# Positions on chip ordered by residue modulo 16, token order restored at the write of the mixed values; the far blocks of pattern 16 transposed in place by VectorE

## The chip, the cores and the metric

One Trainium2 chip, one of its cores. The metric is the device time of one execution in microseconds. TensorE (PE) multiplies; its weight loads are listed apart as PEld. VectorE is DVE, ScalarE is ACT, GpSimd is POOL; all DMAs are issued from SyncE's queue (SP).

## What is computed

One decoder layer on 2048 positions of width 1024, in float32. After a norm, one projection gives q, k, v and a gate for 12 heads of width 64, and four parts for a short convolution:

```python
h = rmsnorm(x, norm_pre_g)
z = einsum('bsd,de->bse', h, w_in)
q, k = rope(q, pos), rope(k, pos)
for window, dilation in ((128, 1), (512, 4), (2048, 16)):
    # regrouped by residue mod dilation: query i sees keys i-128 .. i of its own residue
    o_i, lse_i = dilated_window_attn(q, k, v, window, dilation)
mix_w = softmax(stack(lses), axis=0)
attn_out = sum(mix_w * outs) * silu(g_attn)
conv_out = c_b * causal_depthwise_conv(c_c * c_h, conv_w) * silu(g_conv)
y = concat([attn_out, conv_out]) @ w_out
x = x + rmsnorm(y, norm_post_g)
```

So a query at token t sees three sets of keys: all of the last 129 tokens (pattern 1), every fourth of the last 513 (pattern 4), and every sixteenth of all earlier ones (pattern 16).

## The kernel before, in words

**Tiling.** The 2048 positions are four blocks b of 512 (`NB`, `C`). The columns of the projection are eight groups of 512: groups 0 and 7 are the convolution, groups 1 to 6 are one pair of heads each. One unit n is one group on one block, so there are 32 units, group by group and b from 0 to 3 within each. After them an output projection runs in eight steps with seven products each (L1008 to L1010). Each float32 product is three matmuls of float32r parts, high by high, high by low and low by high; a "part" is made by an ACT copy and a DVE subtraction.

**Positions.** Inside a block the 512 positions stand by residue modulo 4: place = 128 r + i for token 4 i + r (`order`, L52). For pattern 4, residue r is then a contiguous run of 128 places. Pattern 16 lives inside the same score blocks: of the keys of residue r, those with (q - k) % 4 == 0 belong to pattern 16 too (`four`, L60). Patterns 4 and 16 are computed together as kind 4; pattern 1 is kind 1.

**One attention unit** (`attn_unit`, L533). k and q are scaled out of PSUM (L547), their halves are swapped by four small DMAs (L550), and they are rotated by DVE and POOL (L562, L566). k goes to the long-lived tiles `KK` in two parts (L572, L573), q to `Q` (L577, L578); POOL writes a copy `Q1` of q in token order for kind 1 (L582). v is transposed on PE (L594), kept by residue as `V2` and, through two DMAs by way of DRAM (L607, L610), by token as `V1`. `score4` (L623) multiplies `Q` of residue r by all keys of that residue so far, 128 (b + 1) columns; `score1` (L648) multiplies 128 queries of `Q1` by 256 keys that it reads in pieces out of `KK` (L658). DVE adds the mask and takes the row minimum in one pass (L638, L666), ACT does the exponential (L642, L670).

Then `probs` (L677) takes probabilities in groups of up to four 128 x 128 blocks: four PE transposes into PSUM (L684), an ACT copy (L689) and a DVE subtraction (L690) into the tile `pt`, and PE multiplies by v (L703). `gather` (L712) brings the products out of PSUM (L721 to L723). The row minima and sums of kind 1 go through DRAM to the other order (L758, L760); small DVE steps (L769 to L785) make the weights, which go through DRAM to all partitions (L788, L791). DVE weighs both kinds (L807, L808), POOL adds them and multiplies by the gate (L809, L810), and a DMA writes the result to `mix_d` (L811), from where the output projection loads it.

Kind 4 has 4 (b + 1) blocks per head, 40 over the four b; of them 4 (b - 1) for b > 1 lie at least two blocks back. In these far blocks (c < b - 1) every key within pattern 4's window is too old, and only pattern 16 is left: a probability is not zero only where (q - k) % 4 == 0.

**Order.** Nothing is ordered by hand. Every step is given to `Plan` with an engine, an assumed duration, a priority, and what it reads and writes; `Plan.schedule` runs through assumed time and gives each engine the first step that is ready and finds its buffer, and `emit` writes the instructions in that order. A changed step can so move any other. Steps marked `port` are planned so that none of them on DVE stands beside one on POOL. Buffers are rings: `z` (3 PSUM banks, projection), `st` (5 PSUM banks, everything else of attention), `pt` (3), `uu` (4), `u` (1), `xt` (9) and others.

Of the kernel before, what the change touches and what calls it, by code (L numbers as in the profile page):

```python
# [40 lines left out]
def _constants():  # L42
# [18 lines left out]
    tok = (np.arange(128) % 32) * 4 + np.arange(128) // 32  # L61
# [221 lines left out]
def dvet(n):  # L283
    return n / 960.0 + 0.067
# [11 lines left out]
def hybrid_layer(ctx: ExitStack, tc: tile.TileContext, x, w_in, w_out, conv_w, g_pre, g_post,  # L296
# [19 lines left out]
    cst = cp.tile([128, 7 * 128], F32, name="cst")  # L316
    ident, mask1, mask4 = cst[:, 0:128], cst[:, 128:384], cst[:, 384:896]
# [6 lines left out]
    e_d = [dram.tile([4, 32, 4, 4], F32, name=f"ed{i}") for i in range(2)]  # L324
    a_d = [dram.tile([32, 4, 128], F32, name=f"ad{i}") for i in range(2)]
# [24 lines left out]
    KK = [ap_.tile([128, 4, NB * 128], F32R, name=f"kk{i}") for i in range(2)]  # L350
# [65 lines left out]
    def x_chunk(b):  # L416
# [19 lines left out]
        for kt in range(KT):  # L436
# [56 lines left out]
    U, T_last = {}, None  # L493

    def conv_unit(n, i, b, zs):
# [16 lines left out]
        add("DVE", 0.25, pe, lambda: vec.tensor_copy(u.ap[:, 0:2, 1:], u.ap[:, 4:6, 0:127]), r=[(u, 1)], w=[(u, 2)])  # L512
# [12 lines left out]
        add("DVE", dvet(C) + 0.07, pr, lambda: vec.scalar_tensor_tensor(g.ap, y.ap, 0.5, g.ap, op0=ALU.mult, op1=ALU.mult),  # L525
            r=[y], w=[g], port=True)
# [6 lines left out]
    def attn_unit(n, p, b, zs):  # L533
# [89 lines left out]
        def score4(r0):  # L623
# [24 lines left out]
        def score1(g0):  # L648
# [28 lines left out]
        def probs(h, kind, blk, O):  # L677
            ps, pt = Tok(st_r), Tok(pt_r)
            m = len(blk)
            pp = P[h, kind]  # L680

            def tr():
                for i, (a, c) in enumerate(blk):
                    nc.tensor.transpose(ps.ap[:, i * 128:(i + 1) * 128], pp.ap[:, a, c * 128:(c + 1) * 128], ident)  # L684
            add("PE", 0.111 * m, pr, tr, r=[(pp, a) for a in sorted({a for a, _ in blk})] + ["cst"], w=[ps, (pt, "hold")])

            def p4():
                return ps.ap[:, :m * 128].rearrange("p (i c) -> p i c", c=128)
            add("ACT", actt(m * 128, True), pr + URG, lambda: act.copy(pt.ap[:, :m, 0, :], p4()), r=[ps], w=[(pt, 0)])  # L689
            add("DVE", dvet(m * 128), pr + URG, lambda: vec.tensor_tensor(  # L690
                pt.ap[:, :m, 1, :], p4(), f(pt.ap[:, :m, 0, :]), op=ALU.subtract), r=[ps, (pt, 0)], w=[(pt, 1)])

            def pv(part):
                for i, (a, c) in part:
                    dst = O[a // 2].ap.rearrange("p (l q) -> p l q", l=2)[:, :, (a % 2) * 128:(a % 2 + 1) * 128]
# [9 lines left out]
            for half in range(2):  # L705
                part = [(i, ac) for i, ac in enumerate(blk) if ac[0] // 2 == half]
# [408 lines left out]
```

## Time and profile before

| | us |
|---|---|
| median of 3 runs | 1218.31 |
| the runs | 1217.93, 1218.31, 1219.98 |
| the profiled execution | 1222.89 |
| its span, first to last instruction | 1220.8 |

The profile is of one execution, and its span is 2.1 us shorter than that execution's device time. Terms of a sum come from the span; a change of the span is then taken off the median of the runs. Matmuls are pipelined, so their listed durations overlap: a stream of them is read by the distance from start to start.

### The profile page before, as it was taken

How to read it: one execution, taken by the hardware profiler on the slowest of the kernel's cores; microseconds unless marked ns; L12 is line 12 of the kernel's file. 1: busy time of each engine (PE TensorE's matmuls, PEld its weight loads, DVE VectorE, ACT ScalarE, POOL GpSimd, SP SyncE). 2: the span in 40 equal slices, each digit the busy share in tenths (PEclk: the TensorE clock that was granted, in tenths of full speed). 3: DMA queues.
4: the chain of work that ended last, by engine and by line, in shares of the span. 5: the costliest groups of instructions: out<-in, count | busy, mean ns of one | idle time of the engine just before them, and what ended most of it. 6: DMA issues, size and time to landing. Idle time of an engine off the chain costs nothing.

```text
span 1220.8 us, 20955 instructions
## 1 busy us (share of the span) xinstructions
PE 1201.8 (98%) x6856; PEld 993.4 (81%) x6856; DVE 916.0 (75%) x2287; ACT 717.9 (59%) x1874; POOL 260.1 (21%) x212
## 2 busy tenths in 40 slices
PE   8999999999999999999999999999999999999997
PEld 6888888888878888788887888788888888777886
DVE  5556477877777787787788867787877759988876
ACT  6533447767557676576667676486676553454443
POOL 0011123322322232222332223222323113000000
PEclk9999999999999999999999999999999999999999
DMA  9989777766777657766877748767678779555452
GB/s 342 343 317 338 269 232 236 234 205 200 240 252 245 205 182 261 240 184 209 260 223 254 243 119 269 232 234 248 199 233 280 213 229 302 174 163 175 136 181 86
DMA packets 155884, 280.39 MB, mean 230 GB/s; under 512 B 31872, under 2 KB 90368, under 8 KB 155776
## 3 DMA queue, kind: packets, MB, share of 16 engines
q1 hardware_dynamic: 155776, 279.06, 69.6%
q8 instruction: 54, 0.88, 0.3%
q14 instruction: 54, 0.44, 0.1%
HBM read 215.36 MB, written 51.05 MB: 218 GB/s over the span
## 4 chain that ended last, share of the span: by engine, by line
PE 84%; DVE 8%; DMA 3%; ACT 2%; issue 1%; SPq 1%; DVEq 0%; ACTq 0%
PE z L848 16%; PE z L850 16%; PE z L849 16%; PE st L703 8%; PE st L684 7%; PE st L631 4%; PE st L659 3%; PE st L1010 2%; PE st L1008 2%; PE st L1009 2%; DMA rp<-rp 1%; PE z L1008 1%; PE z L1010 1%; PE z L1009 1%; ACT p L642 1%
## 5 line engine op out<-in xcount | busy, mean ns | idle before, releaser
L848 PE MATMUL z<-xt,w 128*128 128x512 f32 x960 | 397.1, 414 | 0.0
L850 PE MATMUL z<-xt,w 128*128 128x512 f32 x960 | 377.7, 393 | 0.0
L849 PE MATMUL z<-xt,w 128*128 128x512 f32 x960 | 376.4, 392 | 0.0
L850 PEld LDWEIGHTS z<-xt,w 128*128 128x128 f32 x960 | 180.5, 188 | 40.3
L848 PEld LDWEIGHTS z<-xt,w 128*128 128x128 f32 x960 | 181.2, 189 | 32.7 <-issue 3.4
L849 PEld LDWEIGHTS z<-xt,w 128*128 128x128 f32 x960 | 181.5, 189 | 25.8
L690 DVE TENSOR_TENSOR pt<-st,pt 128x512 fp32r<-128x512 f32 x216 | 142.3, 679 | 48.1 <-ACT pt L689 46.2
L642 ACT ACTIVATE p<-p,sm 128x128 f32<-128x128 f32 (+3 forms) x192 | 105.9, 555 | 73.2 <-DVE sm L638 72.9
L689 ACT CAST pt<-st 128x512 fp32r<-128x512 f32 x216 | 120.0, 579 | 36.0 <-PE st L684 34.1
L703 PEld LDWEIGHTS st<-pt,v 128*128 128x128 f32 x852 | 121.5, 190 | 18.2 <-DVE pt L690 4.9
L703 PE MATMUL st<-pt,v 128*128 128x256 f32 x852 | 133.1, 287 | 2.0 <-DVE pt L690 1.9
L684 PE MATMUL st<-cst,p 128*128 128x128 f32 x852 | 123.1, 275 | 2.4 <-DVE sm L638 1.0
L723 DVE TENSOR_TENSOR uu<-st,uu 64x256 f32<-64x256 f32 x192 | 80.0, 421 | 57.1 <-ACT uu L722 53.5
L684 PEld LDWEIGHTS st<-cst,p 128*128 128x128 f32 x852 | 100.6, 141 | 22.8 <-issue 3.2
L752 POOL TENSOR_TENSOR uu<-uu 128x512 f32<-128x512 f32 x48 | 72.4, 1509 | 209.1 <-DVE uu L723 207.4
L638 DVE CUSTOM_DVE_ANT_0 p<-st,cst 128x128 f32<-128x128 f32 (+3 forms) x192 | 81.8, 487 | 46.7 <-PE st L631 46.4
L721 ACT COPY uu<-st 64x256 f32<-64x256 f32 x192 | 70.2, 368 | 58.7 <-PE st L703 52.3
L670 ACT ACTIVATE p<-p,e 128x256 f32<-128x256 f32 (+1 forms) x192 | 94.9, 499 | 12.4 <-DVE e L666 12.3
L562 POOL TENSOR_TENSOR rp<-rp,cs 128x512 f32<-128x512 f32 x24 | 35.3, 1472 | 225.7 <-DMA rp<-rp 145.4
L666 DVE CUSTOM_DVE_ANT_0 p<-st,cst 128x256 f32<-128x256 f32 (+1 forms) x192 | 66.8, 411 | 20.5 <-PE st L659 20.4
L562 DVE TENSOR_TENSOR rp<-rp,cs 128x512 f32<-128x512 f32 x72 | 55.9, 791 | 23.4 <-DMA rp<-rp 23.0
L722 ACT COPY uu<-st 64x256 f32<-64x256 f32 x192 | 69.6, 367 | 3.2 <-DVE uu L723 0.4
(320 smaller groups left out, 1842.7 us busy)
## 6 DMA issues: line engine op xcount, KB each, us to landing
xt<-xt SPq DMA_DIRECT2D x256, 512.0 KB
cs<-t SPq DMA_DIRECT2D x28, 768.0 KB
raw<-in_w_in SPq DMA_DIRECT2D x59, 256.0 KB
rp<-rp SPq DMA_DIRECT2D x192, 64.0 KB
vd<-v SPq DMA_DIRECT2D x96, 128.0 KB
v<-vd SPq DMA_DIRECT2D x24, 512.0 KB
ab<-ad SPq DMA_DIRECT2D x48, 256.0 KB
mix<-g SPq DMA_DIRECT2D x32, 256.0 KB
```

The lines of the kernel that those rows point to most:

```text
L562: add(e, dur, pr, lambda o=o, a=a, i=i, eng=eng: eng.tensor_tensor(o.ap, a.ap, cs.ap[:, i], op=ALU.mult), r=[cs], w=[o], port=True)
L638: add("DVE", dvet(w) + 0.01, pr + URG, lambda h=h, r=r, P4=P4: vec.tensor_tensor_reduce(P4.ap[:, r, 0:w], ps[h].ap[:, (r - r0) * w:(r - r0 ...
L642: add("ACT", actt(w) + 0.19, pr, lambda h=h, r=r, P4=P4: act.activation(P4.ap[:, r, 0:w], P4.ap[:, r, 0:w], AF.Exp, bias=s4(0, h)[:, r:r + ...
L670: add("ACT", actt(256 - lo[g]) + 0.19, pr, lambda h=h, g=g, P1=P1: act.activation(P1.ap[:, g, lo[g]:], P1.ap[:, g, lo[g]:], AF.Exp, bias=E ...
L684: nc.tensor.transpose(ps.ap[:, i * 128:(i + 1) * 128], pp.ap[:, a, c * 128:(c + 1) * 128], ident)
L689: add("ACT", actt(m * 128, True), pr + URG, lambda: act.copy(pt.ap[:, :m, 0, :], p4()), r=[ps], w=[(pt, 0)])
L690: add("DVE", dvet(m * 128), pr + URG, lambda: vec.tensor_tensor(pt.ap[:, :m, 1, :], p4(), f(pt.ap[:, :m, 0, :]), op=ALU.subtract), r=[ps, ...
L703: mm(dst, v, pt.ap[:, i], start=s, stop=e)
L723: add("DVE", dvet(256), pr + URG, lambda: vec.tensor_tensor(cols(a, lo), o()[lo:lo + 64, 0], cols(a, lo), op=ALU.add), r=[O], w=[(a, (h, h ...
L848: mm(z.ap, w.ap[:, 0, js], xt.ap[:, 0], start=kt == 0, stop=False)
L849: mm(z.ap, w.ap[:, 0, js], xt.ap[:, 1], start=False, stop=False)
L850: mm(z.ap, w.ap[:, 1, js], xt.ap[:, 0], start=False, stop=kt == KT - 1)
```

## The change

The 512 places of a block now stand by residue modulo 16 inside residue modulo 4: token 16 a + 4 s + r stands at place 128 r + 32 s + a (a from 0 to 31). The order comes in with the PE transposes of x, whose identity operand becomes the permutation `perm`. The constants grow by these 128 columns, and the first load of them brings 256 columns where it brought 128.

In a far block, query and key of one residue modulo 16 now lie in one 32 x 32 square on the block's diagonal, and all else is zero. `probs` is split into `parts` and `times`. For far blocks `parts` has DVE transpose the 32 x 32 squares in place in SBUF, which transposes the whole block; the ACT copy and the DVE subtraction then read SBUF instead of PSUM, and no PSUM bank is taken. Near blocks keep the PE transposes. For b > 1, `times` multiplies all blocks of one half of O at once.

```diff
-    order = np.arange(C).reshape(128, 4).T.reshape(-1)
+    order = np.arange(C).reshape(32, 4, 4).transpose(2, 1, 0).reshape(-1)
...
-    KK = [ap_.tile([128, 4, NB * 128], F32R, name=f"kk{i}") for i in range(2)]
+    KK = [ap_.tile([128, 16, NB * 32], F32R, name=f"kk{i}") for i in range(2)]
...
-                nc.tensor.transpose(ps.ap[:, i * 128:(i + 1) * 128], xn[i].ap[:, kt * 128:(kt + 1) * 128], ident)
+                nc.tensor.transpose(ps.ap[:, i * 128:(i + 1) * 128], xn[i].ap[:, kt * 128:(kt + 1) * 128], perm)
...
+    def placed(t):
+        return t.rearrange("p (r s a) -> p r s a", r=4, s=4)
+    def natural(t):
+        return t.rearrange("p (r a s) -> p r s a", r=4, s=4)
...
-        g = silu2(zs[3], t, pe)
+        g = silu2(zs[3], t, pe, natural, placed)
...
-        add("POOL", poolt(C), pr, lambda: pool.tensor_tensor(y.ap, y.ap, bb.ap, op=ALU.mult), r=[bb], w=[y], port=True)
+        add("POOL", poolt(C) + 0.2, pr, lambda: pool.tensor_tensor(natural(yn()), placed(y.ap), placed(bb.ap), op=ALU.mult), r=[y, bb], w=[u], port=True)
...
+        def rows(t):
+            return t.rearrange("p (x g a) -> p g x a", x=16, g=4)
+        def tokens(t):
+            return t.rearrange("p (g x a) -> p g x a", g=4, x=16)
...
+        add("DMA", dmat(512), pr, lambda: nc.sync.dma_start(
+            d.rearrange("r p c -> p r c"), f(v2.ap).rearrange("p r k d -> p r (k d)")), r=[v2], w=[dk], land=3.8)
         for g in range(4):
             add("DMA", 0.5, pr, lambda g=g: nc.sync.dma_start(
-                d[g].rearrange("(r j) c -> j r c", r=4), f(v2.ap[32 * g:32 * g + 32]).rearrange("j r k d -> j r (k d)")),
-                r=[v2], w=[dk + (g,)], land=3.8)
-        add("DMA", dmat(512), pr, lambda: nc.sync.dma_start(f(v1.ap), d.rearrange("g i c -> i g c")),
-            r=[dk + (g,) for g in range(4)], w=[v1], land=5.0)
+                f(v1.ap[:, g]), d.rearrange("r (s g a) c -> g (r s) a c", s=4, g=4)[g]), r=[dk], w=[(v1, g)], land=4.0)
...
-                               KK[j][lo:lo + 64, r, 0:w], start=x == 0, stop=x == 2)
+                               KK[j][lo:lo + 64, 4 * r:4 * r + 4, 0:w // 4].rearrange("p s (c a) -> p c s a", a=32), start=x == 0, stop=x == 2)
...
-                            keys = kk[:, :, k0 + 32:k0 + 64] if lo[g] else kk[:, :, k0:k0 + 64].rearrange("p r (c j) -> p c r j", c=2)
+                            keys = kk[:, :, k0 + 8:k0 + 16] if lo[g] else kk[:, :, k0:k0 + 16].rearrange("p x (c a) -> p c x a", c=2)
...
+                add("DVE", dvet(m * 128) + 0.05, pr, lambda: vec.transpose(src(), src()), w=[(pp, a) for a in tiles])
+                add("ACT", actt(m * 128), pr + URG, lambda: act.copy(dst(0), cut(src())), r=[(pp, a) for a in tiles], w=[(pt, 0)])
+                add("DVE", dvet(m * 128), pr + URG, lambda: vec.tensor_tensor(dst(1), cut(src()), f(dst(0)), op=ALU.subtract),
+                    r=[(pp, a) for a in tiles] + [(pt, 0)], w=[(pt, 1)], port=True)
...
+                if kind == 4 and b > 1:
+                    where = {}
+                    for half in range(2):
+                        rs = range(2 * half, 2 * half + 2)
+                        if b == 3 or half == 0:
+                            where.update(parts(h, 4, [(r, c) for r in (rs if b == 3 else range(4)) for c in range(b - 1)], True))
+                        where.update(parts(h, 4, [(r, c) for r in rs for c in (b - 1, b)]))
+                        times(h, 4, {ac: v for ac, v in where.items() if ac[0] in rs}, O[half])
...
-        add("DMA", 0.5, pr, lambda: nc.sync.dma_start(
-            ad.rearrange("c g f -> g c f"), ar.ap.rearrange("p a b -> p (a b)")), r=[ar], w=[ak], land=2.0)
+        for r in range(4):
+            add("DMA", 0.5, pr, lambda r=r: nc.sync.dma_start(
+                ad[:, r].rearrange("c s a -> s c a"), ar.ap[:, r]), r=[ar], w=[ak + (r,)], land=2.0)
...
-        add("POOL", poolt(C), pr, lambda: pool.tensor_tensor(gs.ap, a4.ap, gs.ap, op=ALU.mult), r=[a4], w=[gs], port=True)
-        add("DMA", dmat(256), pr, lambda: nc.sync.dma_start(mix_d[b][p], gs.ap), r=[gs], w=[("mix", p, b)])
+        add("POOL", poolt(C) + 0.2, pr, lambda: pool.tensor_tensor(natural(a1.ap), placed(a4.ap), placed(gs.ap), op=ALU.mult),
+            r=[a4, gs], w=[a1], port=True)
+        add("DMA", dmat(256), pr, lambda: nc.sync.dma_start(mix_d[b][p], a1.ap), r=[a1], w=[("mix", p, b)])
```

Not shown: the masks are computed for the new order; the rows of kind 1 (`E`, `X`) are regrouped by the same DMAs with other strides, where the load of `X` now takes 512 pieces of 16 bytes instead of 128 of 64; the convolution's shift needs one more small DVE copy per unit; the weighing of kind 4 (L807) reads and writes plain rows, and that of kind 1 (L808) the strided ones.

What stands in the program, engine by engine, moves with the plan. On TensorE 144 of the 852 transposes of `probs` are gone, and all other matmuls are there in the same number. Between the projection's matmuls the program before goes 352 times to other work, the changed one 295 times.

TensorE in the unit of the third pair on block b = 3, where the first products with v stand (`st` is a PSUM bank, `p` a tile of probabilities, `pt` a tile of transposed parts, `cst` the constants, `v` a tile of V2). Before:

```order
L684 MATMUL st_120<-cst,p_182 128x128 x4
L848 MATMUL z_116<-xt_127,w_136 128x512
L849 MATMUL z_116<-xt_127,w_136 128x512
L850 MATMUL z_116<-xt_127,w_136 128x512
L703 MATMUL st_118<-pt_189,v_174 128x2x128
L703 MATMUL st_118<-pt_189,v_171 128x2x128
L703 MATMUL st_118<-pt_189,v_172 128x2x128
L703 MATMUL st_118<-pt_189,v_173 128x2x128
```

And now:

```order
L678 MATMUL st_121<-kk_167,q_170 128x256
L678 MATMUL st_118<-kk_167,q_170 128x256
L740 MATMUL st_119<-pt_189,v_174 128x2x128
L740 MATMUL st_119<-pt_189,v_171 128x2x128
L740 MATMUL st_119<-pt_191,v_172 128x2x128
L740 MATMUL st_119<-pt_191,v_173 128x2x128
```

The transposes stood between score blocks and products, one group of four for each residue; now the products of one residue read two `pt` tiles, one of far and one of near parts, and stand behind the scores of kind 1.

VectorE in the unit of the fourth pair on block b = 2, behind the last mask passes of kind 4 (`ISA` is that pass and its accumulator). Before:

```order
L638 ISA p_183,sm_163<-st_121,cst 128x384
L638 ISA sm_163 128x1
L690 TENSOR_TENSOR pt_191<-st_117,pt_191 128x4x128
L573 TENSOR_TENSOR kk_168<-rp_144,kk_167 128x4x128
L578 TENSOR_TENSOR q_169<-rp_143,q_169 128x512
L690 TENSOR_TENSOR pt_189<-st_118,pt_189 128x4x128
```

And now:

```order
L657 ISA p_183,sm_163<-st_117,cst 128x384
L657 ISA sm_163 128x1
L709 STREAM_TRANSPOSE p_182<-p_182 128x4x128
L709 STREAM_TRANSPOSE p_183<-p_183 128x4x128
L711 TENSOR_TENSOR pt_191<-p_182,pt_191 128x4x128
L685 ISA p_187,e_153<-st_118,cst 128x256
```

Two transposes and a subtraction whose inputs both lie in SBUF now stand ahead of the mask passes of kind 1.

## Rows read from the trace of the kernel before

**Rows 1.** The page's first part, busy time by engine: us, share of the span, instructions.

```profile
PE 1201.8 (98%) x6856; PEld 993.4 (81%) x6856; DVE 916.0 (75%) x2287; ACT 717.9 (59%) x1874; POOL 260.1 (21%) x212
```

**Rows 2.** The page's fourth part, the chain of work that ended last, share of the span by engine.

```profile
PE 84%; DVE 8%; DMA 3%; ACT 2%; issue 1%; SPq 1%; DVEq 0%; ACTq 0%
```

**Rows 3.** What TensorE's matmuls waited for: us in total, times, longest us.

```profile
PE st L442 <- DMA p<-in_x: 3.2, 4, 1.7
PE st L703 <- DVE pt L690: 1.9, 1, 1.9
PE st L1008 <- ACT xt L976: 1.8, 1, 1.8
PE st L821 <- DVE u L501: 1.1, 1, 1.1
PE st L684 <- DVE sm L638: 1.0, 2, 0.7
PE st L684 <- DVE e L666: 0.7, 4, 0.2
PE st L684 <- ACT p L642: 0.6, 2, 0.3
```

**Rows 4.** The timeline of TensorE in the units of the fourth pair on blocks b = 2 (the first four rows) and b = 3: start us, us, engine, line, operation; x is how many in a row.

```profile
664.07 0.39 PE L850 MATMUL z<-xt,w 128*128 128x512 f32 x1
664.30 1.04 PE L684 MATMUL st<-cst,p 128*128 128x128 f32 x8
665.09 0.48 PE L848 MATMUL z<-xt,w 128*128 128x512 f32 x1
665.41 0.39 PE L849 MATMUL z<-xt,w 128*128 128x512 f32 x1
...
682.07 0.39 PE L848 MATMUL z<-xt,w 128*128 128x512 f32 x1
...
682.75 0.39 PE L848 MATMUL z<-xt,w 128*128 128x512 f32 x1
...
683.20 0.40 PE L850 MATMUL z<-xt,w 128*128 128x512 f32 x1
683.44 0.60 PE L684 MATMUL st<-cst,p 128*128 128x128 f32 x4
683.79 0.48 PE L848 MATMUL z<-xt,w 128*128 128x512 f32 x1
684.11 0.39 PE L849 MATMUL z<-xt,w 128*128 128x512 f32 x1
```

**Rows 5.** Groups of VectorE's and ScalarE's instructions by line and shape: count | busy us, mean ns of one | idle time before them, and what ended it. `raw`, `w`, `rp`, `cs`, `t` and `pa` lie in SBUF, `st` in PSUM.

```profile
L690 DVE TENSOR_TENSOR pt<-st,pt 128x512 fp32r<-128x512 f32 x204 | 136.1, 686 | 46.8 <-ACT pt L689 45.0
L562 DVE TENSOR_TENSOR rp<-rp,cs 128x512 f32<-128x512 f32 x72 | 55.9, 791 | 23.4 <-DMA rp<-rp 23.0
L410 DVE TENSOR_TENSOR w<-raw,w 128x512 fp32r<-128x512 f32 x59 | 40.1, 694 | 15.8 <-ACT w L409 13.8 <-DMA raw<-in_w_in 1.7
L638 DVE CUSTOM_DVE_ANT_0 p<-st,cst 128x512 f32<-128x512 f32 x48 | 30.4, 687 | 9.8 <-PE st L631 9.6
L638 DVE CUSTOM_DVE_ANT_0 p<-st,cst 128x128 f32<-128x128 f32 x48 | 10.6, 287 | 2.0 <-PE st L631 1.9
L785 DVE STREAM_TRANSPOSE t<-pa 128x128 f32<-128x128 f32 x24 | 7.5, 312 | 0.8
...
L689 ACT CAST pt<-st 128x512 fp32r<-128x512 f32 x204 | 114.8, 584 | 31.1 <-PE st L684 29.3
L409 ACT CAST w<-raw 128x512 fp32r<-128x512 f32 x59 | 35.3, 619 | 37.5 <-PE z L849 18.5 <-DMA raw<-in_w_in 14.3 <-PE st L849 4.5
```

**Rows 6.** Two DVE lines by themselves (durations in ns, least/median/most), then the timeline of the unit of the fourth pair on block b = 2 (start us, us, engine, line; in brackets the idle time before and what ended it).

```profile
L690 DVE TENSOR_TENSOR pt<-st,pt x216: 537/687/694, 147.5 to 1006.4; 128x512 fp32r<-128x512 f32 x108
...
L562 DVE TENSOR_TENSOR rp<-rp,cs x72: 672/686/1790, 130.1 to 930.7; 128x512 f32<-128x512 f32 x72
...
647.03 1.77 POOL L562 TENSOR_TENSOR rp<-rp,cs 128x512 f32<-128x512 f32 x1 [9.13 <-DMA rp<-rp]
...
647.57 1.78 DVE L562 TENSOR_TENSOR rp<-rp,cs 128x512 f32<-128x512 f32 x1
...
649.27 0.55 DVE L638 CUSTOM_DVE_ANT_0 p<-st,cst 128x384 f32<-128x384 f32 x1
...
649.88 0.44 PE L684 MATMUL st<-cst,p 128*128 128x128 f32 x2 [0.66 <-DVE sm L638]
```

**Rows 7.** Busy time of each engine in three stretches of 20 us: the attention of block b = 2, of b = 3 (both fourth pair), and of b = 2 of the next pair. Columns: the stretch, its us, then busy us (instructions) of PE, PEld, DVE, ACT and POOL, the granted clock, the DMA share, GB/s.

```profile
648.00:668.00 20.00, 18.84 (x126) 15.24 (x125) 18.39 (x47) 17.18 (x48) 6.74 (x6) 1.00 0.81 301
670.00:690.00 20.00, 20.00 (x119) 16.11 (x118) 15.40 (x43) 14.21 (x36) 3.74 (x4) 1.00 0.56 156
790.00:810.00 20.00, 19.13 (x128) 15.48 (x127) 18.40 (x47) 17.13 (x47) 6.41 (x6) 1.00 0.84 306
```

**Rows 8.** The timeline of TensorE in the unit of the first pair on block b = 1: 24 score matmuls of kind 4, whose keys are one run of 256, and 24 of kind 1, whose keys are eight runs of 32; each pair of them runs side by side on the two halves of the array.

```profile
173.73 1.70 PE L631 MATMUL st<-kk,q 64*128 64x256 f32 x24
175.36 0.50 PE L848 MATMUL z<-xt,w 128*128 128x512 f32 x1
...
178.99 1.71 PE L659 MATMUL st<-kk,q 64*128 64x256 f32 x24
180.62 0.66 PE L684 MATMUL st<-cst,p 128*128 128x128 f32 x4
```

**Rows 9.** POOL's copy of q and its last product (durations in ns, least/median/most), one wait of DVE for the weights (us in total, times), and TensorE's first transposes on the timeline.

```profile
L582 POOL CAST q<-q x48: 606/614/1134, 136.7 to 936.6; 128x512 fp32r<-128x512 f32 x48
...
L810 POOL TENSOR_TENSOR g<-uu,g x24: 1287/1296/1783, 185.6 to 1032.9; 128x512 f32<-128x512 f32 x24
...
  DMA ab<-ad: 1.4, 1
...
5.39 1.06 PE L442 MATMUL st<-cst,p 128*128 128x128 f32 x8 [0.50 <-DMA cst<-in_consts]
```

More of the change, by code (lines that the diff above doesn't have):

```diff
@@ L323, in hybrid_layer @@
     v_d = [dram.tile([4, 128, 256], F32, name=f"vd{i}") for i in range(2)]
-    e_d = [dram.tile([4, 32, 4, 4], F32, name=f"ed{i}") for i in range(2)]
-    a_d = [dram.tile([32, 4, 128], F32, name=f"ad{i}") for i in range(2)]
+    e_d = [dram.tile([4, 128, 4], F32, name=f"ed{i}") for i in range(2)]
+    a_d = [dram.tile([32, 4, 4, 32], F32, name=f"ad{i}") for i in range(2)]
     z_r = ring(psum, "z", 3, [128, C])
@@ L475, in x_stream, with silu2 @@
         streams.append(add("DMA", dmat(512), n * 100 - 20 + kt, lambda: nc.sync.dma_start(f(s.ap), xt_d[n % NB][kt]), r=[("xt", n % NB, kt)], w=[s]))
-    def silu2(z, t, pr):
+    def silu2(z, t, pr, way=lambda a: a, placed=lambda a: a):
         g, th = Tok(g_r), Tok(rp_r)
-        add("DVE", dvet(C), pr, lambda: vec.tensor_tensor(g.ap, z.ap, t.ap[:, 2], op=ALU.mult), r=[z, t], w=[g])
+        add("DVE", dvet(C), pr, lambda: vec.tensor_tensor(way(g.ap), placed(z.ap), placed(t.ap[:, 2]), op=ALU.mult), r=[z, t], w=[g])
         add("ACT", actt(C), pr, lambda: act.activation(th.ap, g.ap, AF.Tanh, scale=0.5), r=[g], w=[th])
@@ L674, in score1, with parts, src, dst @@
                     ps + [(P[h, 1], "hold") for h in range(2)], rest)
[L677 to L695, printed above, removed]
+        def parts(h, kind, blk, far=False):
+            pt, m, pp = Tok(pt_r), len(blk), P[h, kind]
+            tiles = sorted({a for a, _ in blk})
+            if far:
+                def src():
+                    return pp.ap[:, tiles[0]:tiles[-1] + 1, 0:(b - 1) * 128]
+                def dst(l):
+                    return pt.ap[:, :m, l].rearrange("p (a c) q -> p a c q", c=b - 1)
+                def cut(a):
+                    return a.rearrange("p a (c q) -> p a c q", q=128)
+                add("DVE", dvet(m * 128) + 0.05, pr, lambda: vec.transpose(src(), src()), w=[(pp, a) for a in tiles])
+                add("ACT", actt(m * 128), pr + URG, lambda: act.copy(dst(0), cut(src())), r=[(pp, a) for a in tiles], w=[(pt, 0)])
+                add("DVE", dvet(m * 128), pr + URG, lambda: vec.tensor_tensor(dst(1), cut(src()), f(dst(0)), op=ALU.subtract),
+                    r=[(pp, a) for a in tiles] + [(pt, 0)], w=[(pt, 1)], port=True)
+            else:
+                ps = Tok(st_r)
+                def tr():
+                    for i, (a, c) in enumerate(blk):
+                        nc.tensor.transpose(ps.ap[:, i * 128:(i + 1) * 128], pp.ap[:, a, c * 128:(c + 1) * 128], ident)
+                add("PE", 0.111 * m, pr, tr, r=[(pp, a) for a in tiles] + ["cst"], w=[ps, (pt, "hold")])
+                def p4():
+                    return ps.ap[:, :m * 128].rearrange("p (i c) -> p i c", c=128)
+                add("ACT", actt(m * 128, True), pr + URG, lambda: act.copy(pt.ap[:, :m, 0, :], p4()), r=[ps], w=[(pt, 0)])
+                add("DVE", dvet(m * 128), pr + URG, lambda: vec.tensor_tensor(
+                    pt.ap[:, :m, 1, :], p4(), f(pt.ap[:, :m, 0, :]), op=ALU.subtract), r=[ps, (pt, 0)], w=[(pt, 1)])
+            return {ac: (pt, i) for i, ac in enumerate(blk)}
@@ L696, in pv, with times @@
+        def times(h, kind, where, O):
+            def pv():
+                for (a, c), (pt, i) in sorted(where.items()):
+                    dst = O.ap.rearrange("p (l q) -> p l q", l=2)[:, :, (a % 2) * 128:(a % 2 + 1) * 128]
                     if kind == 4:
@@ L704, in probs @@
             vs = [V2[p * NB + c] for c in range(b + 1)] if kind == 4 else [V1[p * NB + c] for c in range(max(b - 1, 0), b + 1)]
-            for half in range(2):
-                part = [(i, ac) for i, ac in enumerate(blk) if ac[0] // 2 == half]
-                if part:
-                    attn_last.append(add("PE", mmt(256) * len(part), pr, lambda part=part: pv(part), r=[(pt, 0), (pt, 1)] + vs, w=[O[half]]))
+            attn_last.append(add("PE", mmt(256) * len(where), pr, pv,
+                                 r=[(pt, l) for pt in {pt for pt, _ in where.values()} for l in range(2)] + vs, w=[O]))
         UU = {}
@@ L745, in attn_unit @@
                 O = [Tok(st_r), Tok(st_r)]
-                for i in range(0, len(bl), 4):
-                    probs(h, kind, bl[i:i + 4], O)
+                if kind == 4 and b > 1:
[6 more added lines that the diff above has]
+                        times(h, 4, {ac: v for ac, v in where.items() if ac[0] in rs}, O[half])
+                else:
+                    for i in range(0, len(bl), 4):
+                        where = parts(h, kind, bl[i:i + 4])
+                        for half in range(2):
+                            part = {ac: v for ac, v in where.items() if ac[0] // 2 == half}
+                            if part:
+                                times(h, kind, part, O[half])
                 for half in range(2):
@@ L756, in attn_unit @@
         ed, ek = e_d[u % 2], ("ed", u % 2)
-        for r in range(4):
-            add("DMA", 0.5, pr, lambda r=r: nc.sync.dma_start(
-                ed[:, :, r].rearrange("g j c -> j g c"), E.ap[32 * r:32 * r + 32]), r=[E], w=[ek + (r,)], land=2.9)
-        add("DMA", 0.5, pr, lambda: nc.sync.dma_start(
-            X.ap.rearrange("p r c -> p (r c)"), ed.rearrange("g j r c -> (g j) (r c)")), r=[ek + (r,) for r in range(4)], w=[X], land=3.0)
+        for g in range(4):
+            add("DMA", 0.5, pr, lambda g=g: nc.sync.dma_start(
+                ed.rearrange("r (s g a) c -> g (r s) a c", s=4, g=4)[g], E.ap[:, g]), r=[E], w=[ek + (g,)], land=2.9)
+        add("DMA", 0.5, pr, lambda: nc.sync.dma_start(X.ap, ed.rearrange("r p c -> p r c")), r=[ek + (g,) for g in range(4)], w=[X], land=3.0)
         wk = Tok(sm_r)
```

58 lines of the change are left out of this document (28 added, 30 removed).

## The prediction

> **What bounds the kernel now.** I read the busy times first, then the chain, then what TensorE waited for, and last how much time one visit to the transposes takes from the stream of projection matmuls. TensorE is busy for 98% of the span, and the next engine, VectorE, for 75% [rows 1]. Matmuls overlap in the record, so that alone isn't proof; the chain that ended last is: 84% of it runs along TensorE, and 8% along VectorE [rows 2]. TensorE's matmuls waited 3.2 us for the first x, and behind that the longest waits are single ones of 1.9 us and less, for transposed parts, for a form of the output projection and for mask passes [rows 3]; the seven rows shown come to 10.3 us. So almost every microsecond taken out of TensorE's list shortens the run, as long as the others keep up. Here they must carry what TensorE loses.
>
> **What is removed from TensorE.** Far blocks per head: four on block b = 2 and eight on b = 3, so 12 x 2 heads x 6 pairs = 144 transposes, 36 groups of four. Their price is the distance between starts. Projection matmuls follow each other at 227 ns (three from 682.07 to 682.75 [rows 4]). From the L850 at 683.20 to the second matmul behind a visit of four transposes, at 684.11, it is 0.91 us; two paces, 0.455, are the stream's own, so four transposes as a visit of their own cost 0.455 us. The same reading for eight (664.07 to 665.41) gives 1.34 - 0.455 = 0.885 us [rows 4], so four more in a visit cost 0.43. The 36 groups are worth 36 x 0.43 to 0.455 = 15.5 to 16.4 us; I take **16.0**. The products with v, the scores and the projections keep their number and columns and cost what they did.
>
> **What VectorE gets.** First, 36 transposes of 512 columns. The trace has one of 128 columns, at 312 ns; a DVE pass from PSUM grows from 287 to 687 ns between 128 and 512 columns, 400 ns for 384 [rows 5]. So a far transpose takes about 0.71 us, an estimate from these three rows, and 36 take 25.6. Second, 36 subtractions go from one PSUM input to two SBUF inputs. By their own lines nothing changes: 686 ns from PSUM, 694 for the weights' parts from SBUF [rows 5]. But where POOL runs beside them it does. The rotation, with both inputs in SBUF, has a median of 686 ns, a mean of 791 and a longest of 1790, while the longest L690 is 694. One such case in full: POOL starts a product at 647.03, DVE's L562 starts at 647.57 and ends with it after 1.78 us, the mask pass behind it starts at 649.27, and TensorE waits 0.66 us for that pass [rows 5, 6]. The mean gives +0.1 us for each of the 36, 3.8 us; the longest would give 36 x 1.1 = 40, which I don't take, since steps marked `port` are planned apart from POOL and the mean of L562 already holds what planning lets through. In all DVE gets 26 to 29 us, 916 -> about 944 of some 1206, 78%.
>
> [...]
>
> ScalarE's 36 copies read SBUF instead of PSUM, 619 against 584 ns [rows 5]: +1.3 us on an engine at 59% [rows 1], hidden.
>
> **Where that is not hidden.** Over the span DVE has a quarter of its time free, but not everywhere. In the 20 us of attention on b = 3 it is busy for 15.4; four transposes and the held subtractions (4 x 0.8 = 3.2 us) fit. On b = 2 it is busy for 18.4 of 20 [rows 7]. There two transposes and two subtractions add 1.4 to 1.6 us, which would just fill it, while TensorE's own work in the stretch becomes shorter by eight transposes, 0.9 us. So there DVE wants 0.7 to 0.9 us more than TensorE leaves, in six units, 4.2 to 5.4 us, if nothing can be moved out. What waits is queued behind the two transposes in DVE's order: the mask passes of kind 1, which free the PSUM banks for TensorE. On the other hand the neighbouring stretches have room, and 36 fewer PSUM banks are asked for. Bounds: 0, and all of it, 29. I take **3 us** lost, somewhat over half of the 4.2 to 5.4, since it lies nearest to the b = 2 rows.
>
> **The small edits.** At the start TensorE waited 0.50 us for the identity [rows 9], whose load doubles from 64 to 128 KB; at the 301 GB/s of a stretch full of transfers [rows 7] that would be 0.2 us, so **+0.2**. POOL's last product of a unit and the convolution's now write with a stride of four elements, 32 instructions; no row shows such a write. Between the 1.29 us of now and twice that it would cost POOL, at 21% [rows 1, 9], up to 41 us beside other work; nothing of TensorE waits for it within a unit, and I take 0 on the path. POOL's copy of q reads and writes runs of 8 where they were 32: from 614 ns to twice that at most [rows 9], ahead of the scores of kind 1, which stand late in a unit; 0. The three more DMA issues in each unit for the weights, 72 in all, stand on SP ahead of the stream of x; the weights made DVE wait once, 1.4 us [rows 9]; 0 to 2 us, and I take 0. The shorter forms of that chain (L807 without strides) and the doubled small copy in the convolution come to under 1 us either way.
>
> **The sum** against the profiled execution: -16.0 + 3.0 + 0.2 = -12.8 us on a span of 1220.8, so 1208.0. That execution took 1222.89 us and the median of the runs is 1218.31; the same difference off the median gives **1205.5 us**.
>
> **The rivals.**
> (a) *VectorE becomes the bound on b = 2 and b = 3.* For it: 92% of the 20 us on b = 2 and the case in rows 6. Against it: the free 4.6 us on b = 3 [rows 7] and TensorE's short waits up to now [rows 3]. If between 35% and 70% of the 29 us is exposed, 10 to 20 us, the time is 1218.3 - 15.8 + 10 to 20, so 1212 to 1222; in the middle 1216.
> (b) *Slower than before: the keys of kind 1.* L658 read runs of 32 elements and now reads runs of 8, 32 per 256 columns. 24 matmuls with one run of 256 and 24 with eight runs of 32 take the same, 1.63 and 1.63 us from their start to the next matmul's [rows 8], so seven breaks cost nothing that can be seen; of 31 no row tells. [...] It decides from 13 / 270 = 0.047 us a pair on.
> [...]
> (c) *It brings more than the transposes.* The freed PSUM banks and fewer visits (295 for 352) take away waits: half of the 7 us of waits behind the start [rows 3], and none of the 3 us is lost: 1218.3 - 15.8 - 3.5 = 1199.
> (d) *The transposes leave TensorE, but the plan's new order opens waits elsewhere* (a product that stands too early, an x that comes late): no row can show it; TensorE's two longest waits for its own work, 1.9 and 1.8 us [rows 3], in each of six pairs would be 22 us and end at 1227, one of them at 1216.
>
> **How the numbers follow.** The forecast (1201 to 1211): 0.60. (a) 0.17, (b) 0.06, (c) 0.09, (d) 0.08. A measurement of this kernel tells about 0.2% from no change, 2.4 us: faster is below 1215.9, slower above 1220.7. Faster: 0.60 + 0.09, half of (a) and a third of (d), 0.80; within: a third of (a) and a quarter of (d), 0.08; slower: (b) and the rest, 0.12. The range leaves out (b), the upper part of (a) and (d) and the lower half of (c), under 0.2: 1199.5 to 1216.
>
> **What would show it.** TensorE's transposes in `probs` 708 for 852, with the same 0.43 to 0.455 us for four. The new transposes of DVE at 0.6 to 0.8 us each; at 0.4 they cost half as much, at 1.2 rival (a) wins. The far subtractions with a median near 690 ns and a mean near 0.8 us. DVE at 76 to 80%. In the attention of b = 2, DVE near 95% busy, and TensorE's waits for mask passes or `pt` longer than before by some 3 us over the span. The 24 scores of kind 1 still at 1.6 us: if they take 2.2 us or more, (b) is true. I am wrong if TensorE waits over 10 us more than before, or if score matmuls or products with v cost more a piece.

## The result and the profile after

| | us |
|---|---|
| median of 4 runs after | 1207.68 (1206.54 to 1208.92) |
| median of 4 runs before, beside them | 1219.14 |
| ratio, with its 95% interval | 0.9906 (0.9889 to 0.9923) |
| the same comparison on a second chip (the run after2 below) | 0.9878 (0.9859 to 0.9897) |
| the profiled execution after | 1207.84, span 1206.1 |

The kernel is 11.5 us faster by the medians, 14.4 us on the second chip; the forecast was 12.8 us. The two profiled spans differ by 14.7 us, but the profiled execution of before took 1222.89 us, 3.75 more than the median of its runs in this table.

The page after: busy time by engine (answers [rows 1]) and the chain that ended last ([rows 2]).

```profile
PE 1186.5 (98%) x6712; PEld 983.3 (82%) x6712; DVE 930.9 (77%) x2331; ACT 716.7 (59%) x1874; POOL 266.3 (22%) x212
...
PE 90%; DVE 5%; ACT 2%; issue 1%; DMA 1%; SPq 0%; DVEq 0%; ACTq 0%
```

TensorE has 144 matmul records fewer, and its share of the chain rose from 84% to 90%: it is still the bound, and more purely so. What its matmuls waited for after, all lines (us in total, times, longest; the first seven of before are [rows 3]):

```profile
PE st L740 <- DVE pt L724: 2.6, 3, 2.2
PE z L1053 <- DVE xt L1020: 2.0, 1, 2.0
PE st L446 <- DMA p<-in_x: 1.8, 3, 0.9
PE st L718 <- DVE e L685: 1.8, 2, 1.5
PE st L864 <- DVE u L512: 1.1, 1, 1.1
PE st L740 <- DVE pt L711: 0.9, 1, 0.9
PE st L446 <- DMA cst<-in_consts: 0.7, 1, 0.7
PE st L614 <- DVE rp L574: 0.2, 1, 0.2
```

They come to 11.1 us; before, all lines came to 12.0. The sum did not grow, but its parts changed. The waits for mask passes and for `pt` on VectorE, which the prediction named as the sign of a full VectorE, were 3.6 us before (the lines of `pt`, `sm` and `e` in [rows 3]) and are 5.3 now; in another execution of the changed kernel (after2, below) they are 4.5. So 0.9 to 1.7 us of the 3 are there, and shorter waits for x and in the output projection hide them. They are not where the prediction looked: in the attention of b = 2 only the first pair still waits, and the two longest lie in the unit of the second pair on b = 3:

```profile
404.83 0.66 PE L718 MATMUL st<-cst,p 128*128 128x128 f32 x4 [1.50 <-DVE e L685]
408.62 0.62 PE L740 MATMUL st<-pt,v 128*128 128x256 f32 x3 [2.17 <-DVE pt L724]
```

Stretches of 20 us of the fourth pair show why (columns as in [rows 7]). A stretch must be compared with one at the same place in its unit. The unit on b = 2 starts its scores of kind 4 at 639.7 us before and at 628.9 after. The first line is before, from 0.9 us ahead of that start; the second is after, from the same place; the third is after, from 8.3 us behind the start, as the full stretch of [rows 7] was; the last is after on b = 3.

```profile
638.80:658.80 20.00, 18.84 (x120) 14.21 (x119) 14.21 (x42) 11.42 (x34) 4.74 (x4) 1.00 0.78 274
628.00:648.00 20.00, 20.00 (x124) 15.97 (x123) 16.82 (x53) 14.89 (x44) 3.06 (x4) 1.00 0.71 198
637.20:657.20 20.00, 20.00 (x131) 17.16 (x130) 17.06 (x39) 16.34 (x44) 7.17 (x5) 1.00 0.86 215
662.00:682.00 20.00, 20.00 (x122) 15.62 (x121) 18.85 (x54) 13.67 (x38) 2.34 (x2) 1.00 0.72 217
```

At the start of b = 2 VectorE has more to do, 16.8 us where it was 14.2; in the stretch that was full it is busy for 17.1 us where it was 18.4, though two transposes and two subtractions were added to the unit. The new work came to stand where there was room, and other work moved. On b = 3 it went from 15.4 to 18.9. TensorE has no gap in any stretch of after. Now the new work itself, by groups of one form (busy us, mean ns | idle before):

```profile
L711 DVE TENSOR_TENSOR pt<-p,pt 128x512 fp32r<-128x512 f32 x36 | 27.7, 770 | 1.2 <-ACT pt L710 1.1
L709 DVE STREAM_TRANSPOSE p<-p 128x512 f32<-128x512 f32 x36 | 25.0, 707 | 11.0 <-ACT p L661 11.0
```

Both as forecast: 0.71 us for a transpose, 0.77 us for a subtraction. What did change on TensorE is a line that the diff only re-addresses. The timeline of the same unit as in [rows 8], after:

```profile
179.21 1.89 PE L678 MATMUL st<-kk,q 64*128 64x256 f32 x24
181.03 0.66 PE L718 MATMUL st<-cst,p 128*128 128x128 f32 x4
...
681.49 0.40 PE L893 MATMUL z<-xt,w 128*128 128x512 f32 x1
681.74 0.60 PE L718 MATMUL st<-cst,p 128*128 128x128 f32 x4
682.09 0.48 PE L891 MATMUL z<-xt,w 128*128 128x512 f32 x1
682.40 0.40 PE L892 MATMUL z<-xt,w 128*128 128x512 f32 x1
```

24 scores of kind 1 took 1.63 us from their start to the next matmul's, and now take 1.82 in this unit (1.80 in the same unit of another run, below). At 0.17 us more for 24, the lower of the two, the 540 matmuls of full width (22.5 times 24) cost 3.8 us. It is so in every unit: the 18 with b > 0 read 1.63 to 1.64 us before and 1.77 to 1.83 after, and all 576 matmuls, summed from start to start without waits, 40.0 and 43.5 us, 3.5 more. Four transposes as a visit cost what they did: from the L893 at 681.49 to the second projection behind them 0.91 us, as in [rows 4].

So the trace gives -16.0 for the transposes, +3.8 for the scores and -0.9 for the waits: -13.1 of the 14.7 us between the two spans. Summing every line of TensorE from start to start closes the rest. The transposes went from 81.5 to 68.5 us and the projection that they interrupt from 735.1 to 731.7, together -16.4. The scores of kind 1 are +3.5, the products with v -1.8, the output projection -1.7, the transposes of x and all other lines +1.1, the waits -0.9, and the work behind the last matmul +1.5 (8.4 us where it was 6.9). The terms below 2 us have no cause shown here: another execution of the plan of before (the last experiment) differs from this one by 1.9 us in the projection alone.

### The profile page after: what moved, and what is told of

Same layout as the page of the kernel before. It is cut to its first block, busy times and chain, and to the rows that moved or that the text cites. A ratio compares the mean times of both kernels' runs of the same rounds, so it can differ in the third digit from the quotient of the medians.

```text
span 1206.1 us, 20803 instructions
## 1 busy us (share of the span) xinstructions
PE 1186.5 (98%) x6712; PEld 983.3 (82%) x6712; DVE 930.9 (77%) x2331; ACT 716.7 (59%) x1874; POOL 266.3 (22%) x212
## 4 chain that ended last, share of the span: by engine, by line
PE 90%; DVE 5%; ACT 2%; issue 1%; DMA 1%; SPq 0%; DVEq 0%; ACTq 0%
PE z L891 17%; PE z L893 17%; PE z L892 17%; PE st L740 8%; PE st L718 6%; PE st L650 4%; PE st L678 3%; PE st L1053 2%; PE st L1051 2%; PE st L1052 2%; PE z L1053 2%; PE z L1052 2%; PE z L1051 2%; PE st L893 1%; PE st L891 1%; PE st L892 1%
## 5 line engine op out<-in xcount | busy, mean ns | idle before, releaser
L891 PE MATMUL z<-xt,w 128*128 128x512 f32 x960 | 395.2, 412 | 0.0
L893 PE MATMUL z<-xt,w 128*128 128x512 f32 x960 | 376.8, 393 | 0.0
L893 PEld LDWEIGHTS z<-xt,w 128*128 128x128 f32 x960 | 180.5, 188 | 40.7
L891 PEld LDWEIGHTS z<-xt,w 128*128 128x128 f32 x960 | 181.2, 189 | 36.0 <-issue 6.0
L740 PEld LDWEIGHTS st<-pt,v 128*128 128x128 f32 x852 | 118.3, 189 | 17.4 <-DVE pt L724 5.2
L740 PE MATMUL st<-pt,v 128*128 128x256 f32 x852 | 125.0, 284 | 3.5 <-DVE pt L724 2.6
L724 DVE TENSOR_TENSOR pt<-st,pt 128x512 fp32r<-128x512 f32 (+1 forms) x180 | 117.6, 675 | 11.1 <-ACT pt L723 9.7
L723 ACT CAST pt<-st 128x512 fp32r<-128x512 f32 (+1 forms) x180 | 99.2, 580 | 15.4 <-PE st L718 13.5
L718 PE MATMUL st<-cst,p 128*128 128x128 f32 x708 | 99.8, 274 | 1.8 <-DVE e L685 1.8
L689 ACT ACTIVATE p<-p,e 128x256 f32<-128x256 f32 (+1 forms) x192 | 94.6, 496 | 11.5 <-DVE e L685 11.5
L718 PEld LDWEIGHTS st<-cst,p 128*128 128x128 f32 x708 | 82.2, 140 | 15.9 <-issue 2.8
L685 DVE CUSTOM_DVE_ANT_0 p<-st,cst 128x256 f32<-128x256 f32 (+1 forms) x192 | 66.8, 411 | 24.8 <-PE st L678 24.8
L582 DVE TENSOR_TENSOR rp<-rp,cs 128x512 f32<-128x512 f32 x72 | 59.9, 846 | 20.2 <-DMA rp<-rp 19.6
```

The costliest lines, as they stand in the source:

```text
L582: add(e, dur, pr, lambda o=o, a=a, i=i, eng=eng: eng.tensor_tensor(o.ap, a.ap, cs.ap[:, i], op=ALU.mult), r=[cs], w=[o], port=True)
L689: add("ACT", actt(256 - lo[g]) + 0.19, pr, lambda h=h, g=g, P1=P1: act.activation(P1.ap[:, g, lo[g]:], P1.ap[:, g, lo[g]:], AF.Exp, bias=E ...
L740: mm(dst, v, pt.ap[:, i], start=s, stop=e)
L891: mm(z.ap, w.ap[:, 0, js], xt.ap[:, 0], start=kt == 0, stop=False)
L893: mm(z.ap, w.ap[:, 1, js], xt.ap[:, 0], start=False, stop=kt == KT - 1)
```

## The experiments

Two theories. **S**: the new order makes the scores of kind 1 dearer, 3.5 to 4 us, because their keys are read in short runs, and VectorE gives nothing back. **V**, the prediction's: the order costs nothing, and VectorE, full on b = 2, gives 3 us back. All ratios are to the kernel before on the same chip.

**The order alone.** The condition for the far path never holds:

```diff
-                if kind == 4 and b > 1:
+                if kind == 4 and b > 4:
```

> The new order of the places with every transposition of probabilities left on TensorE, as before (the far path of VectorE is not taken). Theory S (short key runs): the order alone costs TensorE 3.5 to 4 us in the scores of kind 1, and moving the far blocks to VectorE costs TensorE no wait: about 3.7 us more than before, 1222 to 1224 against 1219, and 15 to 16 us more than the changed kernel. Theory V (the prediction's): the order alone costs next to nothing and VectorE on b = 2 gives back 3 us: within 1 us of before, and 12 to 13 us more than the changed kernel.

Measured: 1225.45 us, 1.0059 (1.0046 to 1.0072), so 7.1 us slower than before. The order alone costs, against V, and more than S said. The scores are at their new price:

```profile
179.02 1.87 PE L678 MATMUL st<-kk,q 64*128 64x256 f32 x24
180.82 0.66 PE L718 MATMUL st<-cst,p 128*128 128x128 f32 x4
```

1.80 us for 24, +3.8 us. What else is new is a wait that stands neither in before nor in after, `PE z L891 <- DMA xt<-xt`, 3.4 us in three times, the longest 1.9. All waits come to 13.2 us where before has 12.0, so it is not clear that this wait makes up the whole rest. SyncE's queue shows what stood ahead of x in one of them:

```profile
587.34 2.39 SPq L836 DMA_DIRECT2D ad<-t  x4
589.77 2.46 SPq L806 DMA_DIRECT2D ed<-e  x4
592.39 1.14 SPq L839 DMA_DIRECT2D ab<-ad  x2
593.58 0.58 SPq L479 DMA_DIRECT2D xt<-xt  x1
```

The issue of the weights is four instructions (L836, 2.39 us) where it was one. That would be the term of 0 to 2 us in the prediction, taking effect where the plan puts x behind it; in the changed kernel the projection waits for no x. No run issued the weights in one instruction at the same plan, so this cause is likely and not shown.

Against the changed kernel, which differs by the far path alone, this run takes 18.6 to 22 us more (1.0059 against 0.9906 and 0.9878). That is what the transposes are worth, 16, and some 3 to 6 us that come with this plan's own waits and order.

**Runs of keys in the scores of kind 1**, three lengths at the same plan. The changed kernel reads 32 runs of 8:

```diff
-  keys = kk[:, :, k0 + 8:k0 + 16] if lo[g] else kk[:, :, k0:k0 + 16].rearrange("p x (c a) -> p c x a", c=2)
+  keys = kk[:, 0:4 if lo[g] else 8, b * 32:b * 32 + 32]                                     # 8 runs of 32
+  keys = kk[:, 0:8 if lo[g] else 16, b * 32:b * 32 + 16]                                    # 16 runs of 16
+  keys = kk[:, 0:8 if lo[g] else 16, b * 32:b * 32 + 16].rearrange("p x (c a) -> p c x a", c=4)   # 64 of 4
```

> The changed kernel, but the scores of kind 1 read their 256 key columns as 8 runs of 32 elements (other keys of the same block, so the scores of kind 1 are not the reference's); order, sizes and waits stay. Theory S: 24 such matmuls fall back by 0.15 us to what they took before, 270 pairs give back 3.5 to 4 us: 1203.5 to 1204.5 where the changed kernel takes 1207.7. Theory V: no change, 1207 to 1208.

> As the last, with 16 runs of 16 elements (other keys, scores of kind 1 not the reference's). If each break between runs costs alike, half of the loss stays: about 1206. If only runs of 8 are too short, all is given back: 1204. Theory V: 1207 to 1208.

> As the last, with 64 runs of 4 elements (other keys, scores of kind 1 not the reference's). If each break costs alike, the loss of 3.7 us is doubled: about 1211.5. If a run of 4 halves the stream, each of the 270 pairs costs 0.11 us, 30 us more than without a loss: about 1234. Theory V: 1207 to 1208.

Measured: 1201.57 us, 0.9860 (0.9843 to 0.9877); 1202.24, 0.9868 (0.9853 to 0.9882); 1203.23, 0.9878 (0.9862 to 0.9895). The same unit, in this order:

```profile
176.78 1.71 PE L678 MATMUL st<-kk,q 64*128 64x256 f32 x24
178.42 0.66 PE L718 MATMUL st<-cst,p 128*128 128x128 f32 x4
```

```profile
178.49 1.73 PE L678 MATMUL st<-kk,q 64*128 64x256 f32 x24
180.15 0.66 PE L718 MATMUL st<-cst,p 128*128 128x128 f32 x4
```

```profile
177.27 1.98 PE L678 MATMUL st<-kk,q 64*128 64x256 f32 x24
179.18 0.66 PE L718 MATMUL st<-cst,p 128*128 128x128 f32 x4
```

1.64, 1.66 and 1.91 us for 24, beside 1.80 to 1.82 for runs of 8. With runs of 32 the old price is back, at an unchanged plan: the way the keys are read sets it. In the time, runs of 32 stand 2.2 to 5.6 us below the changed kernel (0.9860 against its two ratios, 0.9878 and 0.9906; each ratio has an interval of some 2 us to either side); S's 3.8 lies between. Runs of 4 should by their rows cost 0.27 x 22.5 = 6.1 us more than runs of 32; the medians show 1.7, the two profiled spans (1201.2 and 1197.4) 3.8. Between these two executions TensorE's waits fell from 9.6 to 7.6 us (the wait for `e`, L685, of 1.2 us is gone), so part of a dearer score is taken out of waits behind it. Runs of 4 are also not slower than the changed kernel (0.9878 against 0.9878 and 0.9906), though their scores take 0.1 us more for 24, 2 us in all. A halved stream, by the 227 ns of a projection matmul of 512 columns [rows 4] some 0.11 us a pair, did not come: 0.28 us for 24 is 0.023 a pair. The price of a score is thus shown by the rows; in the time of a whole run a part of it is lost, and why stays open.

**The changed kernel again, and more work for VectorE.** The transpose is made three times, which ends at the same result, on both far blocks, on b = 2 alone, or on b = 3 alone; or it is left out.

```diff
+  for _ in range(3):            # or: range(3 if b == 2 else 1), range(3 if b == 3 else 1)
   add("DVE", dvet(m * 128) + 0.05, pr, lambda: vec.transpose(src(), src()), w=[(pp, a) for a in tiles])
```

> The changed kernel again, so that the others of this call have it beside them on the same chip: 1206 to 1209 us, 0.989 to 0.992 of before.

> The changed kernel with each of VectorE's 36 transpositions made three times in a row (two cancel each other). VectorE gets 72 x 0.707 = 51 us more. Theory V (VectorE was full on b = 2 and gave back 3 us): in each b = 2 unit 2.8 us and in each b = 3 unit 5.7 - 1.4 us don't fit, 20 to 40 us more, 1228 to 1248. Theory S (VectorE has room and gave nothing back; the loss is in the scores of kind 1): under 5 us more, 1208 to 1213.

> The changed kernel with VectorE's transposition made three times on b = 2 alone, 24 x 0.707 = 17 us more for VectorE, 2.8 us in each of six units. Theory V: b = 2 is the place where VectorE is full, so all 17 us come back: 1222 to 1225. The trace of the changed kernel has VectorE busy for 16.8 of 20 us there and 18.9 of 20 us on b = 3: by that (theory S) b = 2 takes it, and under 5 us come back, 1207 to 1212.

> The same on b = 3 alone, 48 x 0.707 = 34 us more, 5.7 us in each of six units. With 24.9 us for both together: theory V leaves 8 us for b = 3, 1214; theory S puts 20 us or more here, 1225 to 1230, since VectorE has 1.1 of 20 us free there.

> The changed kernel without VectorE's 36 transpositions: the far blocks go into the products untransposed, so the output is not the reference's; copies, subtractions and products stay. VectorE has 25 us less. Theory V: the 3 us that VectorE's fullness cost come back, 1203 to 1204. Theory S: nothing was lost to VectorE, within 1 us of the changed kernel, 1205 to 1207.

The last column is the difference from the changed kernel by the ratios, with its two ratios (0.9878 and 0.9906) as ends and 1218 us for 1.

| kernel | VectorE's transposes | us | ratio | us more than the changed kernel |
|---|---|---|---|---|
| left out | -25 us | 1208.88 | 0.9920 (0.9895 to 0.9944) | 2 to 5 |
| changed kernel again | 0 | 1205.30 | 0.9878 (0.9859 to 0.9897) | |
| three times on b = 2 | +17 us | 1211.62 | 0.9950 (0.9934 to 0.9966) | 5 to 9 |
| three times on b = 3 | +34 us | 1223.64 | 1.0055 (1.0035 to 1.0074) | 18 to 22 |
| three times on both | +51 us | 1230.21 | 1.0098 (1.0078 to 1.0117) | 23 to 27 |

The second column is the number of transposes times 0.71 us. Leaving 25 us of VectorE's work out brings nothing back; the kernel is no faster, rather a little slower. Its plan is another one, with 2.8 us of waits for x of the kind above, so the run alone does not tell what the transposes cost. The waits for mask passes and `pt` are 3.7 us in it, where the changed kernel has 4.5 and 5.3: by that sign 0.8 to 1.6 us, not 3. V falls by that and by the run on b = 2 alone, for which it said 1222 to 1225. The room is not large, though, and it is smaller on b = 3 than on b = 2: of 17 us more on b = 2 a third to a half shows, more than S said, and of 34 us on b = 3 over half. TensorE's first waits with three on b = 3:

```profile
PE st L741 <- DVE pt L725: 4.1, 5, 1.4
PE st L741 <- ACT pt L711: 3.7, 2, 2.3
PE st L741 <- DVE e L685: 2.9, 1, 2.9
```

The products with v wait for parts that stand behind the transposes in VectorE's and ScalarE's order. TensorE's waits there come to 19.6 us in all, 8.5 more than in the changed kernel, so they make up under half of the 18 to 22 us; the rest was not traced. That is rival (a), 34 us of work later than the prediction looked for it, and on the other block. VectorE's share of the span is 79% there and 77% in the changed kernel: the average hardly tells the two apart.

**Far blocks of b = 2 back on TensorE.**

```diff
-                if kind == 4 and b > 1:
+                if kind == 4 and b == 3:
```

> The changed kernel with the far blocks of b = 2 transposed by TensorE again: 48 more transpositions there, 12 groups of 0.43 to 0.455 us. Theory V: on b = 2 the move brought 5.3 us and lost 3, so about 2.3 us more than the changed kernel, 1210. Theory S: the 5.3 us come back in full, 1213.

Measured: 1213.04 us, 0.9943 (0.9923 to 0.9963), 7.7 us above the changed kernel on the same chip. V said 2.3, S 5.3. So the move on b = 2 kept its worth of 5.3 us. The other 2.4 us are mostly waits, 12.1 us in all where the changed kernel on this chip has 10.0; `pt` alone (L724) makes 4.0 against 2.9.

**The keys in runs of 16, order restored behind the scores.** A score reads its keys as they lie, and the mask pass and the exponential restore the order by way of PSUM:

```diff
-  keys = kk[:, :, k0 + 8:k0 + 16] if lo[g] else kk[:, :, k0:k0 + 16].rearrange("p x (c a) -> p c x a", c=2)
+  keys = kk[:, :, k0 + 8:k0 + 16] if lo[g] else kk[:, :, k0:k0 + 16]
...
-  add("DVE", ..., vec.tensor_tensor_reduce(P1.ap[:, g, lo[g]:], ps[h].ap[:, j * 256 + lo[g]:(j + 1) * 256], mask1[:, lo[g]:], ...
+  add("DVE", ..., vec.tensor_tensor_reduce(found(ps[h], j, g), found(ps[h], j, g), mask(g), ...
-  add("ACT", ..., act.activation(P1.ap[:, g, lo[g]:], P1.ap[:, g, lo[g]:], AF.Exp, ...
+  add("ACT", ..., act.activation(by_c(P1.ap[:, g, lo[g]:], g), found_c(ps[h], j, g), AF.Exp, ...
```

> The changed kernel, with the 256 key columns of a score of kind 1 in the order in which they lie (16 runs of 16); the mask pass leaves its result in PSUM in that order, and the exponential reads it from there and writes blocks of 128 again. Output as the reference. Theory S: 24 scores take 1.87 us instead of 2.0, about 3.5 us less: 1204, as long as PSUM banks held by two more steps don't make TensorE wait. If the banks come free too late for the scores that follow, some 0.5 us for each of 24 units comes back, 12 us: 1212 to 1216.

Measured: 1219.08 us, 0.9991 (0.9977 to 1.0006). The scores fell as expected, the gain did not arrive:

```profile
177.25 1.73 PE L693 MATMUL st<-kk,q 64*128 64x256 f32 x24
178.92 0.66 PE L733 MATMUL st<-cst,p 128*128 128x128 f32 x4
...
PE st L755 <- DVE pt L739: 5.4, 4, 2.2
PE st L733 <- ACT p L704: 2.7, 2, 1.5
```

1.67 us for 24 where the changed kernel has 1.80 (the expectation's 1.87 and 2.0 do not come from this reading, but the step between them is the same). But TensorE's waits come to 21 us in all their lines where the changed kernel on this chip has 10, with new ones for the exponential (L704) and for mask passes. Some 3 us saved and 11 lost make 8, of 10.4 us between the two profiled executions; the medians differ by 14 (1219.08 and 1205.30), so nearly half of it stays open.

**Runs of 8 in the kernel before.** Its keys of residue r lie in 512 columns in a row; here it reads every other 8 of a block's 128:

```diff
-  keys = kk[:, :, k0 + 32:k0 + 64] if lo[g] else kk[:, :, k0:k0 + 64].rearrange("p r (c j) -> p c r j", c=2)
+  keys = kk[:, 0:2 if lo[g] else 4, b * 128:(b + 1) * 128].rearrange("p r (x a) -> p r x a", a=16)[:, :, :, 0:8]
```

> The kernel before, unchanged in layout and order, but its scores of kind 1 read their 256 key columns as 32 runs of 8 elements instead of 8 runs of 32 (other keys of the same block, so the scores of kind 1 are not the reference's). Theory S: 24 such matmuls go from 1.85 to 2.0 us as in the changed kernel, and 270 pairs cost 3.5 to 4 us in the time: 1.003 of before. Theory V: nothing, 1.000.

Measured: 1219.08 us, 1.0005 (0.9995 to 1.0015).

```profile
177.20 1.69 PE L659 MATMUL st<-kk,q 64*128 64x256 f32 x24
178.82 0.66 PE L684 MATMUL st<-cst,p 128*128 128x128 f32 x4
```

1.62 us: S fails in its reason. Runs of 8 cost nothing here. What differs is where the next run lies: 64 bytes further in this kernel, 512 bytes in the changed kernel and in the three with 32, 16 and 4. With runs 512 bytes apart, 24 matmuls take this much more than the 1.63 us of before: 0.01 us with 8 runs, 0.03 with 16, 0.17 to 0.19 with 32, 0.28 with 64. So neither property alone sets the price: short runs close together cost nothing, and long runs far apart next to nothing. Runs that are short and far apart fit all of these rows, but no kernel read the same elements in both orders, so this is likely and not shown.

## Why the prediction was right

**The transposes, -16.0.** Right. 144 fewer, and four still cost 0.455 us as a visit.

**VectorE's load.** Right in each piece: 0.707 us a transpose for 0.71, a median of 681 ns and a mean of 770 for the subtraction (forecast 690 and 0.8), its longest 1500 ns where POOL stands beside it (from 649.74, beside POOL's L852 of 1.30 us from 649.39). The total came to 931 us, 13 less than forecast. VectorE's other passes changed their time. Of the 24 small steps of L770, 11 took 1.15 to 1.29 us before, each beside a POOL instruction, and the others 0.17; after (L817) it is 4, at 1.17 to 1.23, and the line falls from 15.5 to 8.3 us. Others rose, the weights' parts from 40.1 (L410) to 46.0 (L414); how the 13 us add up was not shown.

**"I take 3 us lost" on b = 2.** Wrong, the step that failed. The prediction read 92% on b = 2 as a fixed load and laid the new work on top. A plan that moves every step placed it anew: 85% in the same stretch of b = 2, 94% on b = 3. Its sign, longer waits for mask passes and `pt`, came to 0.9 to 1.7 us instead of 3, and mostly to one unit on b = 3; VectorE near 95% busy on b = 2 did not come. Tripling the transposes shows that the limit is real, but beyond the load that was moved.

**Rival (b), the keys.** The price at which it decides, 0.047 us for each of the 270 pairs of full width (540 matmuls), did not come; a small form of it did, 0.17 / 12 = 0.014 us a pair, 3.8 us. The prediction's own sign of being wrong, score matmuls that cost more a piece, thus came true in small. This price took the place of most of the 3 us, so the sum came out right with one term exchanged for another: that is luck. The prediction set the forecast's price at zero since seven breaks cost nothing [rows 8]; 31 breaks, most of them steps of 512 bytes, are another case: 1.80 to 1.82 us for 24 in the changed kernel, where the kernel before with 31 breaks, most of them steps of 64 bytes, takes 1.62.

**The small edits.** The wait for the identity went from 0.5 to 0.7 us, the +0.2 of the sum; but it is anything from 0.2 to 1.7 us in the other runs of the new order, so one trace doesn't confirm the size. With x arriving earlier, both waits together fell from 3.7 to 2.5. POOL's strided product has a mean of 1421 ns (L852; 1398 before), within the forecast, and its copy of q a median of 617 ns (L602; 614 before). TensorE waited for no x behind SyncE's added issues in this plan, and 3.4 us in another.

**Rivals (c) and (d).** Neither: all waits together fell by 0.9 us where (c) took 3.5, and no new one is longer than 2.2 us.

## What to carry over

A busy share in a window is a load only if nothing can move out of it, and two windows compare only at the same place in their unit; with a planner that orders everything, add the new work to the unit's whole period and ask which stretch is full afterwards. When data is laid out anew, price every reader of it on the engine that bounds, even if its line in the code is only re-addressed: here 24 such scores went from 1.63 us to 1.80 to 1.82, with 31 breaks of mostly 512 bytes. A right total can hold two wrong terms: here the rows of the matmuls and the waits told them apart, and the runs that change one reading at the same plan.

## What was not expected of the hardware

- A TensorE operand read in short runs cost by where the runs lie: 24 matmuls of 256 columns took 1.62 us with 32 runs of 8 that lie 64 bytes apart, and 1.80 to 1.82 with 32 runs of 8 that follow at 512 bytes; with 16 runs of 16 at 512 bytes 1.66.
- The convolution's product, which VectorE now writes with a stride of four elements, takes over half as long again: 684 ns before (L481), 1082 now (L485). POOL's product with the same stride took hardly more than before (a mean of 1421 ns for 1398). The prediction had no term for VectorE's; it is off the path, 8 x 0.4 us. The row, a group of one form:

```profile
L485 DVE TENSOR_TENSOR g<-st,cs 128x512 f32<-128x512 f32 x4 | 4.3, 1082 | 0.0
```
